# Moving first-half products, state terms and resident chunks in a fused transformer-block kernel

## The chip, the cores and the metric

The kernel runs on one core of one Trainium2 chip. The metric is the device time of one execution in microseconds (us), as the median of several runs. One execution before the change was also profiled; all rows of the trace below come from it.

## The reference

A block of depth 1 on 1024 tokens of width 1024, all in fp32:

```
h = hybrid_mixer(x)                                  # x @ w_in, four mixers of width 256, @ w_mix_out
x = layer_norm(2**0.25 * x + h)
h = memory_cross_attention(x, mem)                   # 4 heads of 256, 256 memory rows
x = layer_norm(2**0.25 * x + h)
h = (silu(x @ w_gate) * (x @ w_up)) @ w_down         # D_FF = 2816
x = layer_norm(2**0.25 * x + h)
```

The four mixers are dilated attention, retention, gated linear attention (GLA) and an S5 layer. Retention works in chunks of 128 tokens: for each chunk and head `o = (q k^T * decay) v + q R`, with `R` the state carried from earlier chunks. GLA has the same form, with its states in chunks of 64. `(q k^T * decay) v` is called the values term below, `q R` the state term.

## The kernel before, in words

Every projection is computed with operands split in a high and a low part (`split`, lines 146 to 154): ScalarE (ACT) casts the raw operand to a rounded high part, VectorE (DVE) subtracts to get the low part, and `mm3` runs three matmuls on TensorE (PE): high by high, high by low, low by high. The weights pass through `wraw` (3 buffers, filled by DMAs on the queue of SP) into `whi` and `wlo` (4 buffers each). TensorE's order is the order of the program text (`pinned`); the order on the other engines and queues is set by a scheduler that plays the program through at build time, and is fixed then.

Most larger tiles, 128 x 1024 fp32, come from one pool of 37 buffers (`big`, line 131; `C4 = 37`). Each `big` writes two columns by a memset on GpSimd (POOL), and these memsets stand in the order of the calls: a memset waits until the buffer that it is given is free, and the later ones wait behind it. Smaller 128 x 512 tiles come from a pool of 4 (`half`).

**Retention and GLA** (`retention`, `gla`): for each tile of 128 tokens `scores(tt)` computes q k^T for 4 heads into PSUM (matmuls on 64 rows by 128 columns of the array), DVE multiplies by the decay or copies under a mask, `values(tt)` multiplies by v (128 rows by 64 columns) and then adds the state terms (64 rows by 64 columns) into the same PSUM columns; `head_turn` copies them out, `head_part` transposes (`ob`). `weave` puts matmuls of other projections (`rv`, `fm`, `kt`) between these groups.

**Gate and up** (`ffn`, `gu_first`, `gu_rest`): a Strassen-like scheme with 7 products for each of 11 pairs of column blocks, each product 24 matmuls of 128 x 512. `gu_first(i)` runs the products B11 and B21 (PSUM names `gc`) and leaves `e1` (a `big` tile, `ge`) and `h` (a `half` tile). `gu_rest(i)` runs T1, T2, B22, T3, T4 in that order (names `gb`, `ga`, `gb`, `ga`, `ga`), DVE evicting each into `q`, `u` and `e1` (`gq`, `gu2`, `ge`), and POOL forms differences that go to DRAM for the down projection (`st`, names `hA`, `hS`): S3 reads `h` and `u`, S1 reads `u` and `q`, S2 reads S1 and `h`, S4 reads `e1` and S2. The operand `x` stands in SBUF for the whole stage in seven versions of 4 `big` tiles each (`xv`). The weights of T1, T2 and T3 are sums of quarters of the weight matrix: `gu_stream` loads quarters r11, r12 into `wraw` and r21, r22 into `big` tiles (`gr`), and POOL forms s1 = r21 + r22 and s2 = s1 - r11 in two more (`gs`), then T3's and T4's weights in place. The stream runs two products ahead of TensorE, and asks for the `gr` and `gs` tiles of pair i + 1 at product T3 of pair i. From pair 2 on `down_sums` takes two more `big` tiles a pair (`dw`), and POOL forms four differences of the down weights.

The first `NFIRST` pairs run `gu_first` all before `gu_rest(0)`; the others run it just before their own `gu_rest`. The four tiles `g0` and the pair `qu` serve pair 0.

**Down** (`product`, `keep`): six products of 11 chunks, here D1 to D6; a chunk is 12 matmuls on one raw tile that two DMAs fill. D1 and D4, D5 write the PSUM banks `dr`, D2, D3 and D6 `da`. D5 adds onto the banks in which D4 stands, after DVE has read D4 out of them (`add`, line 784). A seventh product, D7 (`dn`), runs at the end from 11 resident chunks (`kept`, `dv`), which `keep` loads and splits in between; the tuple given to `product` names the chunks behind which one is loaded.

Of the kernel before, what the change touches and what calls it, by code (L numbers as in the profile page):

```python
# [18 lines left out]
P = 128  # L19
# [6 lines left out]
ALPHA = 2.0 ** 0.25  # L26
# [1 line left out]
WCH = 1024  # L28
C4 = 37
NPAIR = NFF // 2  # L30
NFIRST = 3
HV = ("A11", "A12", "A22", "S1", "S2", "S3", "S4")
SUW = 1024 + 3 * P

# [1 line left out]
class Kernel:  # L36
# [634 lines left out]
                         start and k == 0, k == 3, skip_group_check=True)  # L671
            yield m

    def gu_first(self, i, e1=None, mid=None):
        nc, e1 = self.nc, e1 or self.big("ge")
        c, h = [self.bank("gc") for _ in range(2)], self.half("h")
        for m in self.gu_prod(c, "B11", True):
            nc.scalar.copy(out=e1[:, m * 512:m * 512 + 512], in_=c[m])  # L678
        if mid:
            mid()  # L680
        for m in self.gu_prod(c, "B21", False):
            if m:
                nc.vector.tensor_tensor(out=h, in0=h, in1=c[1], op=ALU.mult)
            else:
                nc.scalar.activation(out=h, in_=c[0], func=AF.Silu)
        return e1, h
# [54 lines left out]
    def ffn(self, out):  # L741
        nc = self.nc
        self.vi, self.vs = [], self.gu_stream()
        self.psx.close()
        self.ps = self.psx.enter_context(self.tc.tile_pool(name="pf", bufs=8, space=PSUM, reuse_waits="tile"))
        self.bank = lambda s: self.ps.tile([P, 512], F32, tag="b", name=self.nm(s))
        self.tr = lambda s: self.bank(s).rearrange("p (a b) -> p a b", a=4)
        e = [self.big("ge") for _ in range(NFIRST)]
        f = [self.gu_first(0, e[0])]
        self.xt(6)  # L750

        def mid():
            self.xt(7)
            self.g0 = [self.big(n) for n in ("gr", "gr", "gs", "gs")]
            self.x2_sums()

        f.append(self.gu_first(1, e[1], mid))
        f.append(self.gu_first(2, e[2]))
        for i in range(NPAIR):
            if i >= 2:  # L760
                self.down_sums(i - 2)
            self.gu_rest(i, *(f[i] if i < NFIRST else self.gu_first(i)))
        for i in range(NPAIR - 2, NPAIR):
            self.down_sums(i)
        self.xv = None
        self.X = []
        def more_x(ts):
            for t in ts:
                self.X.append(self.big("X"))
                nc.sync.dma_start(self.X[t], self.xdr[t])  # L770

        more_x(range(4))
        g, b = self.bcast_row("ln_ff_g"), self.bcast_row("ln_ff_b")
        self.vs = self.down_stream([("A12", "B21"), ("A11", "B11"), ("S2", "T2"), ("S1", "T1"), ("S4", "B22"),
                                    ("S3", "T3")])
        hs, X, kept = [slice(0, 512), slice(512, 1024)], self.X, []

        def keep(i):
            raw = self.down_raw(i, "A22", "T4")
            kept.append([self.big("dv", F32R) for _ in range(2)])  # L780
            self.split(*kept[-1], raw)

        def add(x, sl, ps, scale):
            nc.vector.scalar_tensor_tensor(out=x[:, sl], in0=x[:, sl], scalar=scale, in1=ps, op0=ALU.mult, op1=ALU.add)  # L784

        def product(ps, start, evict, ahead=()):
            for i in range(NPAIR):
                w = self.next_v()
                if i in ahead:
                    keep(len(kept))  # L790
                for j in range(4):
                    self.mm3(ps[j], [q[:, j * P:(j + 1) * P] for q in w], [q[:, 512:] for q in w],
                             start and i == 0, i == NPAIR - 1, skip_group_check=True)
                    if i == NPAIR - 1:
                        evict(j, ps[j])

        def low(j, ps):
            self.residual(X[j], hs[1], 1, ps, 1.0)
            self.last_norm(j, g, b, out, hs)

        def high(j, ps):
            self.residual(X[4 + j], hs[1], 0, ps, 1.0)
            add(X[4 + j], hs[0], ps, ALPHA)

        r, ac = [[self.bank(n) for _ in range(4)] for n in ("dr", "da")]
        product(r, True, lambda j, ps: add(X[j], hs[0], ps, ALPHA))
        product(ac, True, lambda j, ps: self.residual(X[j], hs[0], 0, ps, 1.0))
        more_x(range(4, 8))
        product(ac, False, lambda j, ps: add(X[j], hs[1], ps, ALPHA), (1, 4, 7, 10))
        r = [self.bank("dr") for _ in range(4)]  # L810
        product(r, True, lambda j, ps: add(X[4 + j], hs[1], ps, ALPHA), (1, 4, 7, 10))
        product(r, False, low, (2, 5, 8))
        product(ac, False, high)
        for j in range(4):
            ps = self.bank("dn")
            for i, q in enumerate(kept):
                self.mm3(ps, [x[:, j * P:(j + 1) * P] for x in q], [x[:, 512:] for x in q], i == 0, i == NPAIR - 1)
            self.residual(X[4 + j], hs[0], 1, ps, 1.0)
            self.last_norm(4 + j, g, b, out, hs[::-1])
# [267 lines left out]
    def retention(self):  # L1087
        nc = self.nc
        yield from ("rk", "rv")
        k, v = self.t["rk"], self.t["rv"]  # L1090
# [3 lines left out]
        R = self.big("R")  # L1094
# [15 lines left out]
        for tt in range(NT - 1):  # L1110
            if tt + 1 < NT - 1:
                keys(tt + 1)
            o = kdt[tt // 4][:, (tt % 4) * 256:(tt % 4 + 1) * 256]
            for h in range(4):
                c = tt * P + (h // 2) * 64
# [18 lines left out]
        def scores(tt):  # L1134
            sl = slice(tt * P, (tt + 1) * P)
            s = self.two("rs").rearrange("p (a n) -> p a n", a=2)
            for h in range(4):
                r = slice(64 * (h % 2), 64 * (h % 2) + 64)
                c = (h // 2) * P
                self.mm(s[:, h % 2, c:c + P], k[h // 2][r, sl], q[h // 2][r, sl], start=True, stop=True)  # L1140
            w = self.half("rw")
            nc.vector.tensor_tensor(out=w.rearrange("p (a n) -> p a n", a=2), in0=s[:, :, :256],
                                    in1=dec[:, :512].rearrange("p (a n) -> p a n", a=2), op=ALU.mult)
            st[tt] = s, w

        def values(tt):
            sl = slice(tt * P, (tt + 1) * P)
            s, w = st.pop(tt)
            for i in range(2 if tt else 1):
                for h in range(4):  # L1150
                    a, j = h % 2, h // 2
                    r, c = slice(64 * a, 64 * a + 64), (a * 2 + j) * P
                    o, z = s[64 * j:64 * j + 64, a, 256:384], tt * P + j * 64
                    if i:
                        self.mm(o, R[r, z:z + 64], q[j][r, sl], start=False, stop=True, tile_position=(64 * a, 64 * j))
                    else:
                        self.mm(o, v[tt][:, h * 64:(h + 1) * 64], w[:, c:c + P], start=True, stop=tt == 0,
                                tile_position=(0, 64 * j))
            st[tt] = self.head_turn(s)

        def back(tt):
# [24 lines left out]
    def gla(self):  # L1186
# [81 lines left out]
        def scores(tt):  # L1268
            sl = slice(tt * P, (tt + 1) * P)
            s = self.two("gs").rearrange("p (a n) -> p a n", a=2)  # L1270
            for h in range(4):
                r = slice(64 * (h // 2), 64 * (h // 2) + 64)
                self.mm(s[:, h // 2, (h % 2) * P:(h % 2 + 1) * P], ke[r, sl], qi[h % 2][r, sl], start=True, stop=True)
            w = att[:, (tt % 2) * 512:(tt % 2) * 512 + 512]
            nc.vector.copy_predicated(out=w.rearrange("p (a n) -> p a n", a=2),
                                      mask=self.gla_mask.rearrange("p (a n) -> p a n", a=2), data=s[:, :, :256])
            st[tt] = s, w

        def values(tt):
            s, w = st.pop(tt)  # L1280
            for h in range(4):
                a, j = h // 2, h % 2
                self.mm(s[64 * j:64 * j + 64, a, 256:384], v[tt][:, h * 64:(h + 1) * 64], w[:, h * P:(h + 1) * P],
                        start=True, stop=False, tile_position=(0, 64 * j))
            for e in range(2):
                for h in range(4):
                    a, j = h // 2, h % 2
                    r, c = slice(64 * a, 64 * a + 64), (2 * tt + e) * 64
                    self.mm(s[64 * j:64 * j + 64, a, 256 + 64 * e:320 + 64 * e], R[r, c:c + 64], qi[j][r, c:c + 64],
                            start=False, stop=e == 1, tile_position=(64 * a, 64 * j))  # L1290
            st[tt] = self.head_turn(s)

        def back(tt):
# [511 lines left out]
```

## Time and profile before

| what | value |
|---|---|
| median of 3 runs | 1444.9 us (1444.57 to 1445.55) |
| profiled execution, own time | 1443.19 us |
| profiled execution, span | 1441.4 us |
| TensorE matmul busy | 1405.3 us, 97% of the span |
| VectorE, ScalarE, GpSimd busy | 916.7, 518.7, 330.6 us |
| mean granted TensorE clock | 0.995 of full speed |

The span runs from the first to the last instruction; the profiled execution's own time is 1.8 us longer, and 1.7 us below the median of the runs. Times in the trace count from the start of the span. Retention and GLA run from 303 to 437 us, gate and up from 786 to 1215, the down projection from 1215 to the end.

### The profile page before, as it was taken

The numbers are of one execution on the slowest core, as the hardware profiler recorded it, in microseconds if no ns is written. First come the engines' busy times: TensorE is split into PE (matmuls) and PEld (weight loads), VectorE is DVE, ScalarE is ACT, GpSimd is POOL, SyncE is SP. The second block draws the span as 40 slices with busy tenths as digits, with TensorE's granted clock in tenths as the row PEclk, the third lists the DMA queues.
The fourth block names the chain that finished last, engine by engine and source line by source line (L and its number), as shares of the span: only waits on it lengthen the run. The fifth ranks groups of instructions, "written<-read, shape, count | busy, mean of one in ns | idle before, by whom it ended". The sixth has DMA issues, their size and how long they took to land.

```text
span 1441.4 us, 20876 instructions
## 1 busy us (share of the span) xinstructions
PE 1405.3 (97%) x7802; PEld 1155.9 (80%) x7802; DVE 916.7 (64%) x1632; ACT 518.7 (36%) x818; POOL 330.6 (23%) x588
## 2 busy tenths in 40 slices
PE   8999999999999999999999999999999999999897
PEld 6876787788787888888888877788888888888786
DVE  7986455465566398557548977666655545556585
ACT  5223434522344133443335612222232332354442
POOL 2000000100000000000000357766667674000022
PEclk9999999999999999999999999999999999999999
DMA  7442011000557013125214345455454458667742
GB/s 258 132 133 88 30 45 41 34 31 3 176 190 254 30 30 106 55 77 170 76 44 140 116 133 190 160 179 172 168 167 151 157 187 332 195 217 239 228 151 88
DMA packets 76404, 193.61 MB, mean 134 GB/s; under 512 B 9088, under 2 KB 9872, under 8 KB 76304
## 3 DMA queue, kind: packets, MB, share of 16 engines
q1 hardware_dynamic: 74576, 189.15, 39.5%
q10 hardware_dynamic: 1728, 3.15, 0.6%
q8 instruction: 61, 1.00, 0.3%
q14 instruction: 39, 0.32, 0.1%
HBM read 147.04 MB, written 45.22 MB: 133 GB/s over the span
## 4 chain that ended last, share of the span: by engine, by line
PE 80%; DVE 9%; DMA 5%; issue 2%; ACT 2%; POOL 1%; SPq 1%; DVEq 0%; ACTq 0%; POOLq 0%
PE ga L71 10%; PE fm L71 7%; PE gb L71 7%; PE gc L71 7%; PE da L71 6%; PE q L71 6%; PE dr L71 6%; PE wo L71 6%; PE mx L71 5%; PE dn L71 2%; PE s L71 2%; DVE wlo L148 2%; PE pv L71 2%; PE rv L71 2%; PE gv L71 1%
## 5 line engine op out<-in xcount | busy, mean ns | idle before, releaser
L148 DVE TENSOR_TENSOR wlo<-wraw,whi 128x1024 fp32r<-128x1024 f32 (+3 forms) x180 | 229.1, 1275 | 119.8 <-ACT whi L147 118.8
L147 ACT CAST whi<-wraw 128x1024 fp32r<-128x1024 f32 (+3 forms) x180 | 186.6, 1038 | 306.8 <-PE mx L71 42.2
L71 PE MATMUL ga<-xv,whi 128*128 128x512 f32 x528 | 164.1, 392 | 4.6 <-DVE gq L693 4.5
L71 PEld LDWEIGHTS ga<-xv,whi 128*128 128x128 f32 x528 | 99.6, 189 | 26.8 <-issue 6.2
L71 PE MATMUL gc<-xv,whi 128*128 128x512 f32 x352 | 108.9, 391 | 0.2 <-ACT ge L678 0.2
L71 PE MATMUL gb<-xv,whi 128*128 128x512 f32 x352 | 108.4, 389 | 0.0
L71 PE MATMUL ga<-xv,wlo 128*128 128x512 f32 x264 | 103.2, 391 | 0.0
L71 PE MATMUL fm<-xh,whi 128*128 128x512 f32 x208 | 85.5, 411 | 0.0
L71 PE MATMUL wo<-whi,oT 128*128 128x512 f32 x256 | 82.1, 394 | 0.0
L71 PE MATMUL fm<-xh,wlo 128*128 128x512 f32 x208 | 81.3, 391 | 0.0
L71 PE MATMUL fm<-xl,whi 128*128 128x512 f32 x208 | 81.3, 391 | 0.0
L71 PE MATMUL mx<-whi,yT 128*128 128x512 f32 x256 | 80.7, 392 | 0.3
L71 PEld LDWEIGHTS gc<-xv,whi 128*128 128x128 f32 x352 | 65.7, 188 | 14.3 <-ACT ge L678 0.6
L71 PEld LDWEIGHTS gb<-xv,whi 128*128 128x128 f32 x352 | 66.1, 188 | 13.7
L71 PE MATMUL gc<-xv,wlo 128*128 128x512 f32 x176 | 68.5, 389 | 0.0
L71 PE MATMUL gb<-xv,wlo 128*128 128x512 f32 x176 | 68.5, 389 | 0.0
L260 POOL TENSOR_TENSOR X<-X,ln_ff_b 128x1024 f32<-128x1024 f32 x7 | 16.7, 2404 | 197.4 <-ACT X L259 197.4
L71 PEld LDWEIGHTS ga<-xv,wlo 128*128 128x128 f32 x264 | 49.8, 189 | 10.5
L71 PEld LDWEIGHTS mx<-whi,yT 128*128 128x128 f32 x256 | 48.1, 188 | 11.0 <-DVE X L352 0.6
L71 PE MATMUL dr<-whi 128*128 128x512 f32 x132 | 52.5, 397 | 4.4 <-DVE X L784 4.4
L71 PEld LDWEIGHTS wo<-whi,oT 128*128 128x128 f32 x256 | 48.1, 188 | 9.7
L71 PE MATMUL dr<-whi,wlo 128*128 128x512 f32 x132 | 52.1, 395 | 0.0
(500 smaller groups left out, 3291.9 us busy)
## 6 DMA issues: line engine op xcount, KB each, us to landing
wraw<-in_w_gu SPq DMA_DIRECT2D x28, 512.0 KB, 4.3
gr<-in_w_gu SPq DMA_DIRECT2D x22, 512.0 KB, 4.5
dw<-in_w_down SPq DMA_DIRECT2D x22, 512.0 KB, 4.0
tT<-dw SPq DMA_DIRECT2D x44, 256.0 KB, 2.0
wraw<-hS SPq DMA_DIRECT2D x44, 256.0 KB, 3.3
wraw<-tT SPq DMA_DIRECT2D x44, 256.0 KB, 3.6
wraw<-hA SPq DMA_DIRECT2D x33, 256.0 KB, 2.9
wraw<-in_w_down SPq DMA_DIRECT2D x33, 256.0 KB, 3.3
```

The lines of the kernel that those rows point to most:

```text
L71: return self.pin(self.nc.tensor.matmul(*a, **k))
L147: return (self.nc.scalar.copy(out=hi, in_=src), self.nc.vector.tensor_tensor(out=lo, in0=src, in1=hi.bitcast(F32), op=ALU.subtract))
L148: self.nc.vector.tensor_tensor(out=lo, in0=src, in1=hi.bitcast(F32), op=ALU.subtract))
L260: nc.gpsimd.tensor_tensor(out=x, in0=x, in1=b, op=ALU.add)
```

## The change

Four edits.

- `NFIRST` goes from 3 to 4: B11 and B21 of pair 3 run before `gu_rest(0)`. Pair 3's `e1` is one more `big` tile that is taken at the start of the stage, and its `h` is a `big` tile too (`gh`), of which half is used. For pair 3 the quarters r11 and r12 are now loaded twice.
- In retention the four state matmuls move from `values(tt)`, behind the values term, to `scores(tt)`, behind the scores; they now start the accumulation and the values term adds onto them.
- The same in GLA, with eight state matmuls.
- The resident chunks are loaded behind chunks 1, 3, 5, 7, 9 of D3, 0, 3, 6 of D4 and 1, 4, 7 of D5, instead of 1, 4, 7, 10 of D3 and of D4 and 2, 5, 8 of D5.

```diff
-NFIRST = 3
+NFIRST = 4
...
-    def gu_first(self, i, e1=None, mid=None):
+    def gu_first(self, i, e1=None, mid=None, h=None):
         nc, e1 = self.nc, e1 or self.big("ge")
-        c, h = [self.bank("gc") for _ in range(2)], self.half("h")
+        c, h = [self.bank("gc") for _ in range(2)], self.half("h") if h is None else h
...
         f.append(self.gu_first(2, e[2]))
+        f.append(self.gu_first(3, e[3], None, self.big("gh")[:, :512]))
...
-        product(ac, False, lambda j, ps: add(X[j], hs[1], ps, ALPHA), (1, 4, 7, 10))
+        product(ac, False, lambda j, ps: add(X[j], hs[1], ps, ALPHA), (1, 3, 5, 7, 9))
         r = [self.bank("dr") for _ in range(4)]
-        product(r, True, lambda j, ps: add(X[4 + j], hs[1], ps, ALPHA), (1, 4, 7, 10))
-        product(r, False, low, (2, 5, 8))
+        product(r, True, lambda j, ps: add(X[4 + j], hs[1], ps, ALPHA), (0, 3, 6))
+        product(r, False, low, (1, 4, 7))
...
+            for h in range(4 if tt else 0):
+                a, j = h % 2, h // 2
+                r, z = slice(64 * a, 64 * a + 64), tt * P + j * 64
+                self.mm(s[64 * j:64 * j + 64, a, 256:384], R[r, z:z + 64], q[j][r, sl], start=True, stop=False,
+                        tile_position=(64 * a, 64 * j))
...
-            for i in range(2 if tt else 1):
-                for h in range(4):
-                    a, j = h % 2, h // 2
-                    r, c = slice(64 * a, 64 * a + 64), (a * 2 + j) * P
-                    o, z = s[64 * j:64 * j + 64, a, 256:384], tt * P + j * 64
-                    if i:
-                        self.mm(o, R[r, z:z + 64], q[j][r, sl], start=False, stop=True, tile_position=(64 * a, 64 * j))
-                    else:
-                        self.mm(o, v[tt][:, h * 64:(h + 1) * 64], w[:, c:c + P], start=True, stop=tt == 0,
-                                tile_position=(0, 64 * j))
+            for h in range(4):
+                a, j = h % 2, h // 2
+                c = (a * 2 + j) * P
+                self.mm(s[64 * j:64 * j + 64, a, 256:384], v[tt][:, h * 64:(h + 1) * 64], w[:, c:c + P], start=tt == 0,
+                        stop=True, tile_position=(0, 64 * j))
...
+            for e in range(2):
+                for h in range(4):
+                    a, j = h // 2, h % 2
+                    r, c = slice(64 * a, 64 * a + 64), (2 * tt + e) * 64
+                    self.mm(s[64 * j:64 * j + 64, a, 256 + 64 * e:320 + 64 * e], R[r, c:c + 64], qi[j][r, c:c + 64],
+                            start=e == 0, stop=False, tile_position=(64 * a, 64 * j))
...
                 self.mm(s[64 * j:64 * j + 64, a, 256:384], v[tt][:, h * 64:(h + 1) * 64], w[:, h * P:(h + 1) * P],
-                        start=True, stop=False, tile_position=(0, 64 * j))
-            for e in range(2):
-                for h in range(4):
-                    a, j = h // 2, h % 2
-                    r, c = slice(64 * a, 64 * a + 64), (2 * tt + e) * 64
-                    self.mm(s[64 * j:64 * j + 64, a, 256 + 64 * e:320 + 64 * e], R[r, c:c + 64], qi[j][r, c:c + 64],
-                            start=False, stop=e == 1, tile_position=(64 * a, 64 * j))
+                        start=False, stop=True, tile_position=(0, 64 * j))
```

## Rows read from the trace of the kernel before

**Rows 1.** Page, part 1: busy us (share of the span) xinstructions.
```profile
PE 1405.3 (97%) x7802; PEld 1155.9 (80%) x7802; DVE 916.7 (64%) x1632; ACT 518.7 (36%) x818; POOL 330.6 (23%) x588
```

**Rows 2.** Page, part 5: group | busy us, mean ns | idle before it, what ended most.
```profile
L71 PE MATMUL ga<-xv,whi 128*128 128x512 f32 x528 | 164.1, 392 | 4.6 <-DVE gq L693 4.5
...
L71 PE MATMUL dr<-whi 128*128 128x512 f32 x132 | 52.5, 397 | 4.4 <-DVE X L784 4.4
```

**Rows 3.** Windows: stretch and length, busy us (xcount) by engine, clock, DMA share, GB/s.
```profile
821.70:910.30 88.60, 84.08 (x362) 68.50 (x361) 68.38 (x61) 23.15 (x26) 58.39 (x53) 0.98 0.45 151
1339.40:1345.00 5.60, 5.50 (x14) 3.97 (x15) 4.00 (x5) 1.69 (x2) 0.00 (x0) 0.59 0.75 227
391.00:437.00 46.00, 46.00 (x423) 39.05 (x422) 31.04 (x66) 20.69 (x43) 1.25 (x14) 1.00 0.56 194
```

**Rows 4.** Chain that ended last, in order of time: start, us, what.
```profile
887.28 5.44 PE ga L71 x24
...
1305.19 24.49 PE dr L71 x108
...
1371.98 30.19 PE da L71 x132
```

**Rows 5.** Timeline of PE: start, us, line, operation, count, idle before and its releaser.
```profile
845.99 0.77 PE L71 MATMUL ga<-xv,whi 128*128 128x512 f32 x1 [2.31 <-DVE gq L693]
...
1339.48 0.77 PE L71 MATMUL dr<-whi 128*128 128x512 f32 x1 [4.37 <-DVE X L784]
```

**Rows 6.** Timeline of POOL, 829 to 862 us: buffers taken for pairs 1 and 2.
```profile
829.70 0.10 POOL L134 MEMSET gr<- 128x2 f32 x1 [1.04 <-DVE wlo L148]
...
834.30 0.10 POOL L134 MEMSET gs<- 128x2 f32 x1 [1.03 <-DVE xv L148]
836.52 2.39 POOL L628 TENSOR_TENSOR gs<-gr,gr 128x1024 f32<-128x1024 f32 x1 [2.12 <-DMA gr<-in_w_gu]
...
861.99 0.10 POOL L134 MEMSET gs<- 128x2 f32 x1 [4.73 <-DMA hS<-ge]
```

**Rows 7.** Timeline of PE and POOL in pair 8: T4's first matmuls, then S1.
```profile
1133.54 0.62 PE L71 MATMUL ga<-xv,whi 128*128 128x512 f32 x2
...
1135.31 2.21 POOL L693 TENSOR_TENSOR gq<-gu,gq 128x512 f32<-128x512 f32 x1 [0.88 <-DVE gq L693]
```

**Rows 8.** Groups of instructions by form: the split of s1 and s2.
```profile
L148 DVE TENSOR_TENSOR wlo<-gs,whi 128x1024 fp32r<-128x1024 f32 x22 | 41.1, 1868 | 6.1 <-ACT whi L147 6.1
...
L147 ACT CAST whi<-gs 128x1024 fp32r<-128x1024 f32 x22 | 23.1, 1050 | 25.1 <-PE ga L71 10.0 <-POOL dw L134 7.4 <-POOL gs L628 3.5
```

**Rows 9.** Timeline of ACT in D3 and D4: the first and the last of 26 casts.
```profile
1278.66 1.04 ACT L147 CAST whi<-wraw 128x1024 fp32r<-128x1024 f32 x1
...
1333.88 1.05 ACT L147 CAST whi<-wraw 128x1024 fp32r<-128x1024 f32 x1 [1.36 <-DVE wlo L148]
```

**Rows 10.** Timeline of DVE at the border of D4 and D5.
```profile
1337.51 1.23 DVE L148 TENSOR_TENSOR dv<-wraw,dv 128x1024 fp32r<-128x1024 f32 x1 [1.32 <-ACT dv L147]
1338.65 0.68 DVE L784 SCALAR_TENSOR_TENSOR X<-X,dr 128x512 f32<-128x512 f32 x1
1339.25 1.22 DVE L148 TENSOR_TENSOR wlo<-wraw,whi 128x1024 fp32r<-128x1024 f32 x1
```

**Rows 11.** Timeline of PE in retention: one tile's values and states, and a pair of transposes alone.
```profile
410.32 0.38 PE L74 MATMUL ob<-ident,oT 128*128 128x128 f32 x2
410.63 0.67 PE L71 MATMUL rs<-rw,rv 128*64 128x128 f32 x8
411.23 0.45 PE L71 MATMUL rs<-rq,R 64*64 64x128 f32 x8
411.61 0.39 PE L71 MATMUL kt<-memh,whi 128*128 128x256 f32 x1
...
424.84 0.38 PE L74 MATMUL ob<-ident,oT 128*128 128x128 f32 x2
424.98 0.36 PE L71 MATMUL kt<-memh,whi 128*128 128x256 f32 x1
```

## The prediction, made before the change was run

> **What bounds the kernel now.** I read the page first. TensorE is busy for 97% of the span [rows 1], so time can only come from two places: matmuls that go away, and time in which TensorE waits or runs at its lower clock. The change removes no matmul. The page's groups then show where TensorE waits: the two lines to see are the idle columns, 4.6 us before `ga` matmuls and 4.4 us before `dr` matmuls, both ended by DVE [rows 2]. These two are what edits 1 and 4 can win.
>
> Next, the windows and the chain, for what the waits cost with all that follows. One gate/up product of 24 matmuls takes 5.44 us undisturbed [rows 4], 0.227 us a matmul. Between 821.7 and 910.3 us stand the 15 products of `gu_rest(0)` to `gu_rest(2)`, which need 15 x 5.44 = 81.6 us of the 88.6 [rows 3]: 7.0 us are lost there. Three waits of T4 for DVE's eviction of T3 make up 4.5 of them [rows 2], the first of 2.31 us [rows 5]; the other 2.5 are matmuls at a lower granted clock behind the waits (mean 0.98 of the stretch [rows 3]) and hand-offs. In the down stage D4 starts at 1305.19 and D6 at 1371.98 [rows 4]. Two products of 132 matmuls need 59.9 us; 66.8 pass, so 6.9 us are lost. 4.37 are one wait of D5 for DVE's `add` on D4 [rows 5]. Most of the rest is the clock: from 1339.4 to 1345 us it is granted at 0.59 on average, between its two levels of 1.2 and 2.4 GHz, and 14 matmuls take 5.6 us [rows 3] in place of 14 x 0.227 = 3.2, which is 2.4 us.
>
> Between 391 and 437 us, in retention, TensorE is busy for 46.00 of 46.00 us [rows 3]: no wait there can be shortened.
>
> **Edits 2 and 3, the state terms.** The same matmuls run in another place, for 7 tiles of retention (the first has no state) and 8 of GLA. No wait is on TensorE's path, so only the cost of changing the shape in which the array is used counts. The rows show it: two transposes take 0.14 us when full-array matmuls follow (424.84 to 424.98) and 0.31 when the values term on 128 x 64 follows (410.32 to 410.63) [rows 11], so a change of the column shape alone costs 0.17 us. Before, a tile changes shape into scores and out, into values, from values to states, and out: five changes. After, it is into scores, from scores to states, out, into values, out: five again. Scores and states both use 64 rows, and that change (64 x 128 to 64 x 64) stands nowhere in the trace. Bounds: nothing saved if it costs as the column change above, 0.17 us a tile saved if it is free, 15 x 0.17 = 2.5 us in all; the other way the dearest case is as much again, +2.5. I take -0.2 us, near nothing, since the nearest row is a change of columns alone.
> The Trainium skill (TensorEngine Tiling (Array Packing), Tiling Modes, Key Properties) says that a change of tiling mode, not just of tile, drains TensorE. Rows 11 agree, with 0.17 us a change. By it the sum of these edits is 0; by the reading that only the rows count it would be -2.5.
> The moved matmuls also come before DVE's read of the scores in the same PSUM banks. At worst DVE starts later by the length of the state run, 0.38 us (411.23 to 411.61 [rows 11]); scores stand a tile ahead of their values, so this is hidden.
>
> **Edit 1, the fourth pair.** It moves two products, 10.9 us, ahead of `gu_rest(0)`; the sum of the matmuls stays. On SP it adds the second load of r11 and r12 of pair 3, two transfers hidden under a stage whose DMA share is 0.45 [rows 3]. The T4 waits of before came from work for pairs 1 and 2 on POOL and DVE that fell on T3's eviction, so for pair 0 the wait goes.
>
> What decides is the pool of 37 buffers. The seven operand versions hold 28, and 9 are left. Before, when pair 1 asks for its `gr`, `gr`, `gs`, `gs`, the 9 are: three `ge`, pair 0's `q` and `u`, and these four. It just fits, and rows 6 show the last of them taken at 834.30 as soon as an operand tile comes free. s1 of pair 1 is summed at 836.52 and is in two parts some 841.8 (2.39, 1.05 and 1.87 later [rows 6, 8]), before its T1, which comes at 821.7 + 5 x 5.44 = 848.9 or later. Pair 2's last `gs` had to wait for a store of pair 0 [rows 6], and had time to.
> After, four `ge`, `gh`, `q` and `u` are 7. Two are left, for the two `gr`; both `gs` must wait until pair 0 gives back a tile. The first can be `u`, which S1 reads. So T1 of pair 1 now hangs on this chain, counted from T4's first matmul of pair 0: S1 ends 1135.31 + 2.21 - 1133.54 = 3.98 us after it [rows 7] (a pair where POOL had no older work); memset 0.10 and sum 2.39 [rows 6]; cast 1.05 and split 1.87, the mean [rows 8]; together 9.4. T4 itself takes 5.44, and T1 needs the low part from its third matmul, 0.45 later: 5.9. TensorE waits 3.5 us, where before the chain had 7 us to spare. S2 ahead of the sum on POOL would add at most as much as S1's 2.21, so the bounds are 2.9 (a split of 1.22 [rows 10]) and 5.7. Then the clock falls, as it did behind the other waits: between 0.3 us (a short wait) and the 2.4 above; I take 1.6. That is 5.1 us. DVE and the queue of POOL stand behind the same memset; what is queued there is s2 and its split, due one product later, and the differences of pair 1.
>
> Later pairs have 5 to 7 of the 9 buffers instead of 7 to 8, and from pair 2 on `dw` takes two of them; POOL was already busy for 58 of 88.6 us [rows 3]. So T2 of pairs 1 and 2, T1 of pair 3 and the T4s can wait too, 0 to 6 us together; I take 2.7. Sum of the stage after: 5.1 + 2.7 = 7.8 against 7.0 lost before, **+0.8 us**, between -3.8 and +7.1.
>
> **Edit 4, the resident chunks.** Why does D5 wait? DVE's `add` on D4 (1338.65) stands behind the split of a resident chunk (1337.51) [rows 10], the one loaded behind D4's chunk 10. Edit 4 takes that chunk away from there. But the raw tiles are late as a whole: 26 casts in a row take 1333.88 - 1278.66 = 55.2 us [rows 9], 2.2 us each, and the three raw buffers allow no more. TensorE takes 2.72 us a chunk, and with one resident chunk for every three has only 2.0 us a raw tile. What is saved up runs out just at the end of D4. Both placements have eight resident chunks in D3 and D4 together. After, all eight stand ahead of D5's second chunk, before seven. So that chunk's cast comes one raw tile later, 1333.88 + 2.2 = 1336.1, its split ends at 1338.4, and the `add` that now stands behind it starts 0.25 us before its old place; the next split (1339.25) and the other three adds hardly move. But part of the lateness now falls on single chunks of D4, at most 1.8 us, and the rest at the border, so that no single wait is 4.4 us long and the lower clock's 2.4 us mostly go. Bounds: 0 (all waits as before) and -6.9 (the border is free). I take **-2.0 us**. Each kept chunk costs as many casts, splits and DMAs as before.
>
> **Sum.** +0.8 - 2.0 - 0.2 = -1.4 us. The profiled execution has 1443.2 us with what lies around its span, so 1441.8; the runs' median is 1.7 above it, so 1443.5 us. This kernel's measurement tells 0.2%, 2.9 us, from no change.
>
> **The rivals.**
> *Forecast, little change.* The wait of T1 of pair 1 takes the place of the T4 waits, the down stage wins a little: 1443.5, own range 1442 to 1447.8. Chance 0.44.
> *Faster.* The buffers come free in time (T1 of pair 1 waits 2.9 us with a short spell at the lower clock, the later pairs do not wait: 3.2 lost instead of 7.0, -3.8), which with -2.2 from the rest is -6.0, 1438.9: chance 0.19. Or the D5 border comes free for most of its 6.9 (-5.0), with +0.8 and -0.2 -4.4, 1440.5: chance 0.14. For them: the T4 waits did come from DVE's order, and the resident chunk did stand in front of the `add`. Against them: the count of buffers and the raw rate. Together 0.33.
> *Slower.* The shortage of buffers goes on: 5.7 + 2.4 for T1 of pair 1 and 6 for later pairs, 14.1 lost instead of 7.0, +7.1, with -1 from the rest 1451. It decides once gate/up loses more than 12 us (7.0 + 2.9 + the 2.2 from the rest). For it: `gh` and pair 3's `ge` stay until `gu_rest(3)`. Against: from pair 3 on the chains had slack again. Chance 0.23.
> *No effect in the mixers* is part of the forecast; if the change of columns were free there, any case moves by -2.5.
>
> **How the numbers follow.** Faster by over 0.2% (below 1442) holds the two faster cases, 0.33; slower (above 1447.8) the last, 0.23; within it 0.44. The range leaves out a tenth at each end: 1439 to 1449.5.
>
> **What would show it.** A wait of TensorE of 3 to 5 us at T1 of pair 1, ended by the split of `gs`, with a `gs` memset on POOL waiting for S1 or a store; no wait at T4 of pair 0. In the down stage small waits inside D4 and one of 1 to 3 us at D5, and a clock near 1. In the mixers the matmuls of a tile take as long in sum as before. I am wrong if pair 1's `gs` is taken before pair 0 ends, or if D5 starts without a wait.

## The result, and the profile after

The changed kernel takes 1458.9 us (median of 4 runs, 1455.9 to 1461.9) against 1445.2 (4 runs, 1444.6 to 1445.6): ratio 1.009, interval 1.0072 to 1.0109. It is 13.7 us slower, outside the range of the prediction and on the other side of the one forecast. The profiled execution is one of 1460.4 us, with a span of 1458.7 us, 17.3 longer than before.

I look first at where the 17.3 us are. Gate and up run from 789.4 to 1231.5, 442.0 us; before, from the same rows of the chain, 786.7 to 1215.3, 428.6: +13.4. The stages ahead of it are 2.7 longer; two waits for DMAs in the S5 layer near 90 us, 3.1 us together instead of 2.1, and a lower clock behind them (mean 0.93 from 60 to 110 us, before 1.00) make 3.7 us, and 1.0 is won back behind them. Up to 309 us the order of the instructions on every engine is the same in both kernels, so this is no work of the change. The down stage is 1.1 longer. The page's groups (busy us, mean ns, then idle before them and what ended most of it):

```profile
L71 PE MATMUL ga<-xv,whi 128*128 128x512 f32 x528 | 163.0, 390 | 0.8 <-DVE gq L693 0.7
L71 PE MATMUL gc<-xv,whi 128*128 128x512 f32 x352 | 111.4, 398 | 7.7 <-ACT ge L678 7.6
...
L71 PE MATMUL gb<-xv,whi 128*128 128x512 f32 x352 | 110.2, 395 | 2.3 <-ACT whi L147 2.3
...
L71 PE MATMUL gb<-xv,wlo 128*128 128x512 f32 x176 | 69.8, 397 | 2.0 <-DVE wlo L148 2.0
...
L71 PE MATMUL dr<-whi 128*128 128x512 f32 x132 | 51.8, 392 | 3.5 <-DVE X L785 3.1
L71 PE MATMUL dr<-wlo,whi 128*128 128x512 f32 x132 | 51.7, 392 | 1.5 <-DVE wlo L148 1.5
```

The idle time before `ga` (the T4s, 4.6 us in [rows 2]) is down to 0.8, as hoped for; 7.7 us before `gc`, the first-half products, and 4.3 before `gb` have come. The windows of the stage (length, busy us by engine, clock, DMA share, GB/s) and TensorE's timeline show the places:

```profile
789.20:840.00 50.80, 47.83 (x212) 38.69 (x210) 45.16 (x54) 28.90 (x43) 9.72 (x16) 0.97 0.40 135
840.00:975.20 135.20, 125.42 (x530) 101.72 (x529) 79.29 (x76) 30.30 (x36) 88.15 (x79) 0.96 0.48 160
975.20:1231.30 256.10, 256.01 (x1129) 211.39 (x1128) 143.82 (x144) 73.91 (x88) 165.88 (x172) 1.00 0.55 188
```

```profile
832.78 0.72 PE L71 MATMUL gc<-xv,whi 128*128 128x512 f32 x2 [2.85 <-ACT ge L678]
...
869.68 0.73 PE L71 MATMUL gb<-xv,whi 128*128 128x512 f32 x2 [2.33 <-ACT whi L147]
872.45 0.80 PE L71 MATMUL gb<-xv,wlo 128*128 128x512 f32 x1 [2.04 <-DVE wlo L148]
...
967.50 1.22 PE L71 MATMUL gc<-xv,whi 128*128 128x512 f32 x2 [4.37 <-ACT ge L678]
```

Three places: B21 of pair 3 (2.85), T1 of pair 1 (2.33 + 2.04) and B21 of pair 4 (4.37). Behind each comes a spell at the lower clock: the mean granted clock is 0.77 from 832.8 to 840.2 us, 0.64 from 872.4 to 880.4 and 0.82 from 967.5 to 975.2. The chain shows the 24 matmuls from 832.78 at 7.37 us and 22 from 872.45 at 7.93, against 5.44 and 22 x 0.227 = 4.99:

```profile
832.78 7.37 PE gc L71 x24
...
872.45 7.93 PE gb L71 x22
```

The first window holds the eight products ahead of `gu_rest(0)`. Before they were six, in 35.2 us (786.5 to 821.7); with two more 46.1 are due, so 4.7 are lost. The second holds 22 products, 119.7 us: 15.5 lost. The third loses 0.4. Together that is 20.6. Before, the stage lost 7.0 from 821.7 to 910.3 [rows 3] and 0.4 from there to its end (56 products in 305.0 us), 7.4 in all; the difference is the 13.4 above but for 0.2.

**T1 of pair 1** is the wait that was forecast. Here are GpSimd's rows for it and for the other two places, then ScalarE's and VectorE's:

```profile
807.75 2.40 POOL L628 TENSOR_TENSOR gs<-gs,wraw 128x1024 f32<-128x1024 f32 x1 [5.76 <-DMA wraw<-in_w_gu]
810.11 3.38 POOL L628 TENSOR_TENSOR gr<-wraw,gr 128x1024 f32<-128x1024 f32 x1
...
815.22 2.75 POOL L628 TENSOR_TENSOR wraw<-wraw,gs 128x1024 f32<-128x1024 f32 x1 [1.69 <-DMA wraw<-in_w_gu]
...
863.52 1.29 POOL L693 TENSOR_TENSOR gq<-gu,gq 128x512 f32<-128x512 f32 x1 [4.15 <-DVE gq L693]
864.87 0.10 POOL L134 MEMSET gs<- 128x2 f32 x1
864.93 1.30 POOL L693 TENSOR_TENSOR s<-gq,h 128x512 f32<-128x512 f32 x1
866.18 2.37 POOL L628 TENSOR_TENSOR gs<-gr,gr 128x1024 f32<-128x1024 f32 x1
...
966.73 0.10 POOL L134 MEMSET ge<- 128x2 f32 x1
```

```profile
826.50 1.06 ACT L147 CAST xv<-xr 128x1024 fp32r<-128x1024 f32 x1 [6.10 <-DVE xr L526]
...
831.20 1.04 ACT L147 CAST xv<-xr 128x1024 fp32r<-128x1024 f32 x1 [0.28 <-POOL xv L134]
832.15 0.58 ACT L678 COPY ge<-gc 128x512 f32<-128x512 f32 x1
...
868.59 1.04 ACT L147 CAST whi<-gs 128x1024 fp32r<-128x1024 f32 x1 [2.56 <-POOL gs L134]
```

```profile
811.15 7.90 DVE L526 TENSOR_TENSOR xr<-xr,xr 128x1024 f32<-128x1024 f32 x3
...
869.66 2.73 DVE L148 TENSOR_TENSOR wlo<-gs,whi 128x1024 fp32r<-128x1024 f32 x1 [0.56 <-ACT whi L147]
```

S1 of pair 0 ends at 864.8, and only then is `gs` taken (864.87); S2 stands ahead of the sum, and cast and split follow: the chain of the prediction link by link. Their sizes differ: S1 took 1.29 where 2.21 was taken, S2 added 1.30 where the sum had none, and the split took 2.73 for 1.87.

**B21 of pair 3** is a place the prediction did not name. B21 adds onto banks that ScalarE must first have copied out (`ge`, 832.15). That copy stands behind casts of `x`'s operand versions, and those wait for VectorE's sums `xr` (line 526). Three of the sums took 7.90 us, because GpSimd's sums of pair 0's weights ran at the same time (807.75 to 818). Those had waited for a raw tile until 18.3 us after the start of the stage: two more weight tiles, pair 3's, now stand ahead of pair 0's quarters in the three raw buffers. In the kernel before this wait ended 8.8 us after the start of the stage, GpSimd had these sums done at 805.4, and VectorE's three took 3.49 from 806.79:

```profile
795.49 3.24 POOL L628 TENSOR_TENSOR gs<-gs,wraw 128x1024 f32<-128x1024 f32 x1 [5.66 <-DMA wraw<-in_w_gu]
...
802.10 3.32 POOL L628 TENSOR_TENSOR wraw<-wraw,gs 128x1024 f32<-128x1024 f32 x1
...
806.79 3.49 DVE L526 TENSOR_TENSOR xr<-xr,xr 128x1024 f32<-128x1024 f32 x3
```

**B21 of pair 4** waits for its `ge` tile, whose memset comes at 966.73, in the midst of a GpSimd without idle time. Whether buffers or GpSimd's load put it there, the trace alone does not say.

In retention a tile of the changed kernel reads

```profile
397.38 0.71 PE L71 MATMUL rs<-rq,rk 64*128 64x128 f32 x8
398.03 0.45 PE L71 MATMUL rs<-rq,R 64*64 64x128 f32 x8
398.40 0.39 PE L71 MATMUL kt<-memh,whi 128*128 128x256 f32 x1
...
399.31 0.67 PE L71 MATMUL rs<-rw,rv 128*64 128x128 f32 x8
399.91 0.39 PE L71 MATMUL kt<-memh,whi 128*128 128x256 f32 x1
```

From start to next start, scores take 0.65, states 0.37 and values 0.60: 1.62 us. Before, 0.64 (401.20 to 401.84), 0.38 and 0.60 [rows 11]: 1.62 too.

In the down stage D4 to D6 take 97.8 us (1321.4 to 1419.2) against 97.0 (1305.2 to 1402.2), where three products without waits need 89.8. The wait of 4.37 at D5 is replaced by six of 0.45 to 1.63 in D4, at D5 and in D6, 6.1 us together, with the clock at full speed (1.00). The other 2.0 of the 8.1 us lost are in the matmuls next to these six waits, which take longer than 0.227 from start to start.

### The profile page after: what moved, and what is told of

Read it like the earlier page. It is cut to its first block, busy times and chain, and to the rows that moved or that the text cites. A ratio compares the mean times of both kernels' runs of the same rounds, so it can differ in the third digit from the quotient of the medians.

```text
span 1458.7 us, 20872 instructions
## 1 busy us (share of the span) xinstructions
PE 1413.4 (97%) x7802; PEld 1160.4 (80%) x7802; DVE 914.4 (63%) x1632; ACT 517.8 (35%) x818; POOL 322.9 (22%) x589
## 4 chain that ended last, share of the span: by engine, by line
PE 76%; DMA 7%; DVE 7%; ACT 3%; POOL 3%; issue 3%; SPq 1%; DVEq 0%; ACTq 0%; POOLq 0%
PE ga L71 9%; PE fm L71 7%; PE gb L71 7%; PE gc L71 6%; PE q L71 6%; PE wo L71 5%; PE mx L71 5%; DMA wraw<-tT 3%; PE da L71 3%; PE dn L71 2%; PE dr L71 2%; DVE wlo L148 2%; PE kt L71 2%; PE p L71 2%; PE s L71 2%
## 5 line engine op out<-in xcount | busy, mean ns | idle before, releaser
L71 PE MATMUL dr<-wlo,whi 128*128 128x512 f32 x132 | 51.7, 392 | 1.5 <-DVE wlo L148 1.5
```

The lines of the kernel that those rows point to most:

```text
L71: return self.pin(self.nc.tensor.matmul(*a, **k))
```

## The experiments

All were timed against the kernel before on the same chip, which took 1444.5 to 1445.7 us there.

**The edits one by one.** `a1_fourth_pair` is the kernel before with edit 1, `a2_states` with edits 2 and 3, `a3_resident` with edit 4; the diffs are those of the change.

> The kernel before with edit 1 alone (fourth pair begun early, its h in a whole tile). Theory 1, edit 1 carries the whole loss through the gate/up stage, which took 13.5 us more in the profiled run: 1456 to 1460 us, with the same three waits of TensorE (B21 of pair 3 about 3 us, T1 of pair 1 about 4.5 us, B21 of pair 4 about 4.5 us). Rival, the loss comes from the edits together (schedule of all stages): under 1451.

> The kernel before with edits 2 and 3 alone (state terms). My prediction's term: 1444.9 (-0.2, no difference to be measured). Rival, that a changed order of the other engines after the mixers shifts waits there: between 1443 and 1448; the wait of about 2.4 us of the v products near 448 us in the kernel before would go, as it did in the profile after.

> The kernel before with edit 4 alone (resident chunks placed anew). My prediction's term: 1443 (-2.0). By the profile after, in which D1 to the end took 227.4 us instead of 226.3: 1445 to 1446.5, with several waits of 0.6 to 1.8 us in D4 to D6 in place of one of 4.4.

Edit 1 alone: 1459.2 us, ratio 1.0096 (1.0081 to 1.0112), with all three waits in its profile (2.54, 2.32 + 2.04, 2.02) and one of 1.32 at T4 of pair 2. Edits 2 and 3 alone: 1445.4, 1.0007 (0.9995 to 1.0019). Edit 4 alone: 1444.8, 0.9996 (0.9986 to 1.0006). So edit 1 carries the whole loss, and the other edits change nothing that can be measured, within some 0.2%. Edit 4's profile has the 4.37 at D5 split up like the changed kernel's, in five waits of 0.75 to 1.20, 4.8 us together; D4 to D6 take 96.5 us there:

```profile
1319.87 0.50 PE L71 MATMUL dr<-wlo,whi 128*128 128x512 f32 x1 [0.76 <-DVE wlo L148]
...
1344.32 0.47 PE L71 MATMUL dr<-whi 128*128 128x512 f32 x1 [1.20 <-DVE X L784]
```

**One buffer more.** The `h` of pair 3 goes into a tile of constants that is dead by then.

```diff
-        f.append(self.gu_first(3, e[3], None, self.big("gh")[:, :512]))
+        f.append(self.gu_first(3, e[3], None, self.wglu.rearrange("p a n -> p (a n)")))
```

> The changed kernel with the h of pair 3 in a tile that is dead by then, so that one more of the 37 buffers is free. Theory 1, shortage of buffers: the wait at T1 of pair 1 (4.4 us and a spell at the lower clock, 6 to 7 us in all) goes, the one at B21 of pair 4 shrinks, the one at B21 of pair 3 stays: 1448 to 1453. Rival, backlog of VectorE and ScalarE behind the operand sums: no buffer helps, 1457 to 1460. Rival, GpSimd is the bound in pairs 1 to 3: T1 of pair 1 is relieved, but the time comes back at B21 of pair 4, 1454 to 1458.

1452.8 us, 1.0054 (1.0035 to 1.0072): 5 us back, by the ratios, and in its profile gate and up take 437.1 us instead of 442.0. The waits at T1 of pair 1 and at B21 of pair 4 are gone, B21 of pair 3 keeps 2.73. But T4 of pairs 1 and 2 now wait (TensorE's timeline):

```profile
890.51 1.19 PE L71 MATMUL ga<-xv,whi 128*128 128x512 f32 x2 [4.37 <-DVE gq L693]
...
922.11 1.03 PE L71 MATMUL ga<-xv,whi 128*128 128x512 f32 x2 [2.03 <-DVE gq L693]
```

For the first, GpSimd's timeline names what is late, pair 2's `gr`, which gets the buffer of pair 0's `ge` once that is stored. Its load, pair 2's sums and their splits follow, and the split of s2 (the second row, VectorE's) is the last thing ahead of VectorE's eviction of T3:

```profile
872.91 0.10 POOL L134 MEMSET gr<- 128x2 f32 x1 [2.23 <-DMA hS<-ge]
...
886.41 3.35 DVE L148 TENSOR_TENSOR wlo<-gs,whi 128x1024 fp32r<-128x1024 f32 x1
```

**Four buffers more, and no sums of pair 0.** Two runs that leave work out. In `a5_four_more` T4's operand version is written over T3's; in `a6_no_sums0` pair 0 uses plain quarters in place of their sums.

```diff
-        self.x2_version("T4", b21)
+        v = self.xv["T4"] = self.xv["T3"]
+        for kp in range(2):
+            self.split(v[0][kp], v[1][kp], b21[kp])
```

```diff
             s1 = new("gs")
+            if i == 0:
+                new("gs")
+                for t in (r21, r22, r12, r21, r22):
+                    yield self.versions(t)
+                continue
             sub(s1, r21, r22, ALU.add)
```

> The changed kernel with T4's operand version written into T3's four tiles, so that four more of the 37 buffers are free (T3's own version is overwritten before use: its product is left out of the result, all splits and matmuls still run). Theory 1, shortage of buffers behind all four waits of the gate/up stage: 1443 to 1447, no wait at T1 of pair 1, at B21 of pair 4 and at the T4s. Theory 2, shortage behind T1 of pair 1 and what follows, while B21 of pair 3 (2.9 us and about 1.7 at the lower clock) waits for operand sums that GpSimd slows: 1447 to 1451, with that wait unchanged.

> The changed kernel with GpSimd's four weight sums of pair 0 left out (its products use plain quarters, so pair 0 is left out of the result; all splits and matmuls still run). Theory 2, those sums fall on VectorE's operand sums and each slows the other (three operand sums took 7.9 us in place of 3.5 in the kernel before): three sums take about 3.5 us, the wait at B21 of pair 3 goes, 1452 to 1456. Rival, the buffers for the operand versions set their pace: the wait of 2.9 us stays, 1457 to 1460.

With four more buffers: 1445.0 us, 1.0001 (0.9988 to 1.0013), nearly all of the loss back. No wait at T1 of pair 1 or B21 of pair 4 is left, and that with all of GpSimd's work still there, so it was buffers and not its load. Of `gc`'s 3.6 us of idle time, 2.96 stand at B21 of pair 3, as Theory 2 said; the time is nevertheless under the range of Theory 2 and in that of Theory 1. Gate and up take 429.7 us, with 5.0 lost ahead of `gu_rest(0)` and 3.2 behind (69 products in 378.6 us). The T4s keep 2.1 us together. The page's groups:

```profile
L71 PE MATMUL gc<-xv,whi 128*128 128x512 f32 x352 | 110.4, 395 | 3.6 <-ACT ge L680 3.6
L71 PE MATMUL gb<-xv,whi 128*128 128x512 f32 x352 | 108.4, 389 | 0.0
```

Without the sums of pair 0: 1451.6 us, 1.0041 (1.0027 to 1.0055), 7 us under the changed kernel, a little more than expected. VectorE's three sums take 3.49 us, the wait at B21 of pair 3 is gone, and the two others stay (2.32 + 2.04 and 4.22). The stretch that took 50.8 us in the changed kernel takes 46.0, which is what was due; gate and up as a whole take 437.7, 4.3 less, so the rest of the 7 us lies outside the stage:

```profile
807.66 3.49 DVE L526 TENSOR_TENSOR xr<-xr,xr 128x1024 f32<-128x1024 f32 x3
```

```profile
787.50:833.50 46.00, 45.88 (x211) 37.63 (x210) 40.10 (x55) 28.84 (x43) 1.20 (x12) 1.00 0.45 154
```

**Pair 0's quarters loaded earlier**, with `h` aside as above: the same cause, with nothing left out.

```diff
         for i in range(NFIRST):
+            if i == NFIRST - 1:
+                first = [load(wt(), 0, q) for q in range(2)]
             for q in range(2):
                 yield self.versions(load(wt(), i, q))
```

> The changed kernel with h of pair 3 in a dead tile, and r11 and r12 of pair 0 loaded before the weights of pair 3's first products; nothing is left out, no other edit. If GpSimd's sums of pair 0 falling on VectorE's operand sums are what made TensorE wait at B21 of pair 3: three operand sums take about 3.5 us, the wait goes, and the time is 4 to 7 us under that of the run with h aside alone (1452.8): 1446 to 1449. Rival, it was the sums' share of the work as such (they were left out in that run) or the raw buffers: 1451 or more.

1450.2 us, 1.0036 (1.0023 to 1.0049): 2.6 under the run with `h` aside by ratio, less than the 4 to 7 expected. The intervals of the two runs overlap, but their profiles say the same, 434.6 us for gate and up against 437.1, all of it ahead of `gu_rest(0)` (48.2 against 50.7). GpSimd's first two sums now end at 801.7, VectorE's take 3.49 and the wait at B21 of pair 3 is gone. What is given back is a wait of 1.89 in the middle of B21 of pair 1. The copy that B21 waits for stands on ScalarE behind the cast of pair 3's first weights, and their raw tile, which now comes behind pair 0's quarters, is late (the last two rows):

```profile
798.28 3.38 POOL L628 TENSOR_TENSOR gr<-wraw,gr 128x1024 f32<-128x1024 f32 x1
```

```profile
811.12 3.49 DVE L526 TENSOR_TENSOR xr<-xr,xr 128x1024 f32<-128x1024 f32 x3
```

```profile
808.90 1.04 ACT L147 CAST whi<-wraw 128x1024 fp32r<-128x1024 f32 x1 [5.96 <-DMA wraw<-in_w_gu]
...
810.48 0.73 PE L71 MATMUL gc<-xv,whi 128*128 128x512 f32 x2 [1.89 <-ACT ge L680]
```

**Raw tiles for the resident chunks.** Two runs on the kernel before: each resident chunk takes its raw tile from the pool of 37, or all of them take one such tile in turn.

```diff
-            raw = self.down_raw(i, "A22", "T4")
+            raw = self.down_raw(i, "A22", "T4", self.big("kr"))
```

> The kernel before, with the raw tiles of the resident chunks taken from the pool of 37 in place of the three raw buffers. Theory: in D3 to D6 the three raw buffers allow 2.2 us a tile and the chunks ask for 2.0, so the lateness of some 6 us falls somewhere whatever the placement, which is why edit 4 won nothing; with raw tiles of their own the resident chunks leave the streamed ones at 2.7 us a tile, the wait at D5 goes and D1 to the end takes some 5 to 6 us less: 1438 to 1441. Rival, VectorE's order (the add behind a split) or the DMAs set it: 1443.5 to 1446, the wait of about 4.3 us at D5 stays.

> The kernel before, with one tile of the pool of 37 as the raw tile of all resident chunks in turn. With a tile for each, D4 to D6 had no wait left, but the chunks were all loaded at once at the start of the down stage, and D1 took 34.3 us in place of 29.9. Theory: with one tile they come one after another, D1 takes 30 and D4 to D6 still have no wait: 1436 to 1439. Rival, one tile is late at D5 as three shared ones were: 1442 to 1445.

With a tile each: 1440.3 us, 0.9961 (0.9946 to 0.9977), faster than both kernels. D4 and D5 run 264 matmuls in 59.93 us, without a wait; before they took 66.8 [rows 4]. D1 takes 34.3 in place of 29.9; the resident chunks are all fetched and split in it, the last by 1238. In its profile the down stage is 2.8 us shorter, half of the 5 to 6 expected; where the rest of the 5.6 us by the ratio lies is not shown. The chain, and the window of D1 with 325 GB/s:

```profile
1310.33 59.93 PE dr L71 x264
```

```profile
1215.90:1250.20 34.30, 32.18 (x134) 25.87 (x134) 28.34 (x26) 20.09 (x20) 3.85 (x15) 0.95 0.90 325
```

With one tile in turn: 1445.1, 1.0003 (0.9988 to 1.0018), a miss. D4 and D5 are free here too, and D1 takes 29.9, but a new wait of 5.83 stands behind D2: VectorE's reads of D2 (line 224) are queued behind the split of a chunk that is being loaded.

```profile
1278.17 1.22 DVE L148 TENSOR_TENSOR dv<-kr,dv 128x1024 fp32r<-128x1024 f32 x1 [2.34 <-ACT dv L147]
1279.31 0.68 DVE L224 SCALAR_TENSOR_TENSOR X<-X,da 128x512 f32<-128x512 f32 x1
```

In both runs the splits of all eleven resident chunks are done before D3 starts (the last begins at 1236.5 and at 1278.2), although the program asks for them in D3 to D5. So D4 and D5 are free of the chunks' raw tiles and of their splits at once. The runs show that the loss in D4 and D5 comes with the resident chunks; they do not tell the shortage of raw buffers from the rival of the order of VectorE's work.

**s2 written over r11**, so that a pair needs one buffer less: on the changed kernel with `h` aside (`a9_s2_raw`), on the kernel before with the one raw tile in turn (`a10_before_s2`), and on the changed kernel with everything together (`a11_all`).

```diff
-            s2 = new("gs")
-            sub(s2, s1, r11)
-            yield self.versions(s1)
             sub(r21, r11, r21)
-            sub(r12, r12, s2)
-            yield self.versions(s2)
+            sub(r11, s1, r11)
+            yield self.versions(s1)
+            sub(r12, r12, r11)
+            yield self.versions(r11)
```

> The changed kernel with the h of pair 3 in a dead tile and s2 of every pair written over its r11, so that a pair needs one buffer less again; nothing is left out. Shortage of buffers as the cause of T1 of pair 1, B21 of pair 4 and the T4s: the 2 waits left at T4 of pairs 1 and 2 (4.4 and 2.0 us) shrink to under 2 together, B21 of pair 3 keeps its 2.9 us, 1446 to 1449. Rival, raw buffers are now held longer and the weights come late: 1452 or more.

> The kernel before with the single raw tile for resident chunks and s2 written over r11. If before's three waits at T4 (4.5 us) come from late buffers too, they shrink and this is 2 to 4 us under the run with the single raw tile alone; if they come from the order of VectorE's work, the two are alike within 1 us.

> The changed kernel with h of pair 3 in a dead tile, s2 over r11, one raw tile for the resident chunks, and r11 and r12 of pair 0 loaded before the weights of pair 3's first products, so that GpSimd's sums of pair 0 come before VectorE's operand sums. By the theories together all four causes are gone: B21 of pair 3 without wait, 1434 to 1439. If the early loads leave the stream a single raw buffer and it falls behind: 1442 or more.

All three missed: 1455.1 (1.008, 1.0059 to 1.0102), 1456.4 (1.0072, 1.005 to 1.0094) and 1452.3 (1.0061, 1.0038 to 1.0084). In `a11_all` B21 of pair 3 has no wait, as expected, but B21 of pair 1 waits 1.69 and T4 of pair 2 waits 7.43 us; in `a9_s2_raw` T4 of pair 2 waits 7.54, in place of the two T4 waits before, and gate and up take 437.1 us as without this edit. VectorE's timeline in `a9_s2_raw`:

```profile
908.68 1.63 DVE L148 TENSOR_TENSOR wlo<-gs,whi 128x1024 fp32r<-128x1024 f32 x1 [6.75 <-ACT whi L147]
...
917.64 1.23 DVE L148 TENSOR_TENSOR wlo<-wraw,whi 128x1024 fp32r<-128x1024 f32 x1 [4.53 <-ACT whi L147]
```

VectorE sits 4.53 us at the split of s2 with T3's eviction behind it, because written over r11, s2 must come after the difference r21, and GpSimd ran that (3.38 us from 909.19) and a down difference first. The experiment put in a new chain, so it tells little of the buffers; nor was the rival tried by itself, that raw tiles held longer make the weights late. Whether the T4 waits of the kernel before come from late buffers stays open: in `a10_before_s2` the one of pair 0 is gone, the one of pair 1 has grown to 3.10, and later pairs wait up to 1.0 each at B21.

## Why the prediction was wrong

**Edit 1, +0.8 us predicted, +14.5 measured alone.** The term was mis-sized; the lost time of the stage came out as 20.6 us (4.7 + 15.5 + 0.4), not 7.8. It has three parts.

*A step that failed: "two transfers hidden under a stage whose DMA share is 0.45".* The share of the DMA engines was the wrong cover to name. What the two tiles of pair 3 take is places in the three raw buffers: pair 0's quarters come behind them, GpSimd's sums move onto VectorE's operand sums, the casts of ScalarE wait for those, and the copy that B21 of pair 3 needs stands behind the casts: 2.85 of wait and 1.9 at the lower clock. Runs without the sums and with earlier loads both remove the wait. That "for pair 0 the wait goes" was right for T4; the wait at B21 of pair 3 is a new one, and the sum had no term for it.

*The wait at T1 of pair 1* was right in place and mechanism: `gs` behind S1, 4.37 us within the bounds of 2.9 to 5.7, S2 ahead of the sum as the upper bound had it. That it came near the 3.5 taken is in part luck, since a shorter S1 and a longer split cancel. The spell behind it cost 2.9 us (7.93 - 4.99), above the bound of 2.4. One buffer more takes the wait away, though T4 of pairs 1 and 2 then wait.

*The later pairs, "0 to 6 us together; I take 2.7",* were taken too small. Of the 15.5 us, 4.37 and 2.9 belong to T1 of pair 1, so 8.2 are left, with B21 of pair 4 the largest (4.37). I had counted buffers for the weights of the later pairs, but not for `ge` of pair 4, whose memset stands in the same order of calls. With four more buffers these waits are gone but for 2.1 us at two T4s.

The rival "The shortage of buffers goes on" had the right mechanism for two of the three waits and too low a price: 14.1 lost against 20.6. Of the 6.5 between them 4.7 are B21 of pair 3, which is no shortage of buffers: with four more it still waits 2.96.

**Edit 4, -2.0 predicted, 0 measured (-0.1% to +0.1%).** The failing step: "the lower clock's 2.4 us mostly go", taken as won. They did go, but the waits did not stay at 4.4 us: they grew to 6.1 in the changed kernel and 4.8 with edit 4 alone, and the matmuls next to them lost 2.0 and 1.9 us more. D4 to D6 lose 8.1 and 6.7 us, where they lost 7.2 before.

Why the waits do not shrink is in part argued. The rate in the prediction, a raw tile every 2.2 us where 2.0 are asked [rows 9], would fix the lateness at the end whatever the order of the loads. The chain of the kernel before bears it out: a transfer issued at 1332.00, as soon as a split has freed a raw buffer, has landed at 1336.35, and its tile is cast at once and split by 1338.74; 6.7 us for each of three buffers are 2.2 us a tile.

```profile
1332.36 3.99 DMA wraw<-tT
...
1336.38 1.05 ACT dv L147
```

The runs with raw tiles from elsewhere removed the whole loss in D4 and D5, but they also moved the resident chunks ahead of D4, so they do not show the rate by itself to be the cause.

**Edits 2 and 3, -0.2 predicted, 0 measured (-0.05% to +0.2%).** This was right: there are five changes of shape before and after, and the run of states costs 0.37 next to the scores as it cost 0.38 next to the values. So in these rows the change from 64 x 128 to 64 x 64, which no row of before showed, is not free. The rule of the Trainium skill (TensorEngine Tiling (Array Packing), Tiling Modes, Key Properties) weighed there, that a change of tiling mode drains TensorE, agrees with this.

## What to carry to other kernels

When work is moved ahead, count what it holds while it waits, in every pool that it passes: the tiles it keeps until its second half, and the places in the load buffers that others now get later. A low share of the DMA engines says nothing about either. And splitting one wait into several is no gain by itself: here five or six short waits cost as much as one long wait with its spell at the lower clock. Taking the extra loads out of D4 and D5 freed these, but 4.4 of the 6.9 us came back in D1, and with a single raw tile all of it in D2 and D3.

## What the runs showed that was not expected

A sum of two SBUF tiles on VectorE took up to 3.43 us in the changed kernel, against 1.22 undisturbed, while GpSimd summed weights: three in a row 7.90 against 3.49. GpSimd's own sums next to them took 2.40 to 3.38. The Trainium skill (SBUF — State Buffer, Who interferes with whom) says that a VectorE instruction with two SBUF inputs contends with a GpSimd instruction that reads SBUF, and that the port pair they share is an exclusive lock. The durations agree, and the two runs that keep the sums apart bring the 3.49 back.
